# Loads without a limit in flight, and empty places that are neither gathered nor scattered, in an experts' layer

## The chip, the cores and the metric

One core of one Trainium2 chip. The time is that of the program on the device in microseconds (us). TensorE (PE in the rows; its weight loads are PEld) multiplies, VectorE (DVE), ScalarE (ACT) and GpSimd (POOL) work element by element, SyncE (SP) issues the plain DMAs, and GpSimd issues the indirect ones. Sixteen DMA engines move the bytes of all of them.

## The reference

A first block (a two-way gated delta rule beside a convolution, then a mixture of experts) and a second block (a state-space branch beside a short convolution, then a dense feed-forward), on 512 tokens of 1024 values in float32. Only the experts matter here:

```python
top_w, top_idx = ...          # 6 of 64 experts for each of 512 tokens, by the router
for e in range(64):           # for the tokens of expert e:
    y = (silu(h[tok] @ w_gate[e]) * (h[tok] @ w_up[e])) @ w_down[e]
    routed[tok] += y * weight[tok, e]
out = x + gt2 * (routed + swiglu(h, s_gate, s_up, s_down))
```

`w_gate[e]` and `w_up[e]` are 1024 x 256, `w_down[e]` is 256 x 1024, so an expert has 3 MB of weights; 512 x 6 = 3072 pairs of token and expert are computed.

## The kernel before

Normalized rows of the 512 tokens are stored in HBM (`hrow`, 640 rows), and two tables of 640 rows in HBM take the results (`yacc`: table 0 starts from x, table 1 from zeros). Rows 512 to 639 of all three stand for "no token".

The host plans 42 blocks (`plan`, L1072) of up to 128 rows. Four fixed experts (60 to 63) have a block each. The other sixty are ranked by their token count on the chip, and each rank has a capacity (`CAPS`, sum 4032): ranks 0 to 17 have blocks of their own (the first three have two each), ranks 18 to 43 share a block in pairs (64 rows each), ranks 44 to 59 in fours (32 rows each). The blocks are numbered in their order of work: 0 to 3 fixed, then fours (4, 9, 12, 14) among the largest single ones, then, from 16 to 41, a pair and a single in turn. `fixed` (L1482) and `table` (L1413) fill, for each part of a block, the list of its tokens from the front; a place that has no token gets 512 plus its row as its number and the weight 0 (L1460, L1461, L1495, L1496). Tokens over a capacity go to extra blocks in a loop with a count that is read at run time (`beyond`, L1670).

A block (`blocks`, L1641, and `ffn`, L1597): the weights of its experts are loaded in parts of 1 MB, three an expert (`load_block`, L1532; `load`, L1501; gate and up are parts 0 and 1, down is part 2). Its rows are gathered from `hrow` by one indirect DMA on GpSimd (`gather`, L1589), two blocks ahead, into one of three buffers X; these are zeroed once at the start. TensorE transposes the rows (`pt_x`), multiplies by gate and up (`gu`, 8 steps; the experts of a pair or a four run side by side on TensorE, so a block takes it as long with one expert as with four), ScalarE and VectorE make h (times the weight of the place), TensorE transposes h (`pt_h`) and multiplies by down (`py`), VectorE scales into y, and GpSimd adds y's rows to a table (`scatter`, L1633), one indirect DMA for each part, with the capacity's rows, the tables in turn. All rows of a block go through this, with or without a token. The shared expert's work is put among the blocks 10 to 16.

The weight parts go round a ring of 1 MB slots (`slot`, L1186): 10 at first, 2 more after `table`, 13 from block 17 on. SP issues the loads in program order. A load waits until its slot's last readers on TensorE are done, and also, by a dependency made by hand (L1523 to L1526, `FLIGHT = 2`), until the load before last has landed. The lines that the steps below speak of: 1522 (a weight load), 1593 (a gather), 1638 (a scatter), 139 and 142 (all matmuls and all transposes), 1217 to 1220 (zero fills), 1673 (the count of extra blocks is read), 2239 (block two reads the tables).

Of the kernel before, what the change touches and what calls it, by code (L numbers as in the profile page):

```python
# [7 lines left out]
F32 = mybir.dt.float32  # L8
# [3 lines left out]
ALU = mybir.AluOpType  # L12
# [111 lines left out]
class Tensor:  # L124


    def __init__(self, tc):
        self.tc, self.eng, self.pin, self.t = tc, tc.nc.tensor, False, 0.0
# [72 lines left out]
class ModWeights:  # L201
# [10 lines left out]
    def load(self):  # L212
        if self.todo:
            j, q = self.todo.pop(0)
            tag, bufs = self.slots[self.n % len(self.slots)]
            self.n += 1
            r = self.rows
            w = self.k.W.tile([P, r, 512], F32, tag=tag, name=f"wm{j}_{q}", bufs=bufs)
            self.k.nc.sync.dma_start(w, self.k.I["w_mod"][j, :, q * r:q * r + r, :])
            self.have.append(w)  # L220
# [24 lines left out]
def mod_vec(k, j, mw, ps, lag=2.6):  # L245
# [6 lines left out]
    t = k.W.tile([P, 4, 2], F32, tag="mt", name=f"mt{j}", bufs=2)  # L252
    nc.vector.tensor_reduce(t, pt.rearrange("p c (g s) -> p c s g", s=32)[:, :, 0:2, :], AX.X, ALU.add)
    nc.vector.tensor_tensor(k.modT[:, 4 * j:4 * j + 4, :], t,
# [803 lines left out]
        50, 49, 46, 45, 44, 44, 43, 42, 41, 41, 40, 39, 38, 37, 37, 32, 32, 32, 31, 30, 30, 28, 26, 25, 23, 22, 20, 20, 18, 17, 16]  # L1058
CAPS = [-(-c // 16) * 16 for c in CAPS]
NOV = 72  # L1060
FLIGHT = 2
LEAVE = 6
LAST = 0
AHEAD = 2
# [82 lines left out]
class Moe:  # L1147


    def __init__(self, k, es, pool):  # L1150
        self.k = k
        nc, tc = k.nc, k.tc
        self.hrow = k.dram.tile([640, 1024], F32, name="hrow")

        self.yacc = [k.dram.tile([640, 1024], F32, name=f"yacc{i}") for i in range(2)]
        self.nsc = sum(len(w) for _, _, w in BLOCKS)
        self.keep = pool(es, "moek", 1)
        self.gt2 = k.gt2 = self.keep.tile([P, 1024], F32, name="gt2")
        self.wt = {}
        self.order = []  # L1160
        self.slots = []
# [28 lines left out]
    def open_route(self, es, pool):  # L1190

        k, nc = self.k, self.k.nc
        V = nc.vector
        self.sp = pool(es, "shared", 1, side="right")
        self.er = ExitStack()
        self.rp = rp = pool(self.er, "route", 1, side="right")
        self.es = ExitStack()
        self.scp = sp = pool(self.es, "score", 1, side="right")
        keep = self.keep
        self.tok = keep.tile([P, NBT], I32, name="tok")  # L1200
        self.tw = keep.tile([P, NBT], F32, name="tw")
        self.tok2 = keep.tile([32, NB], I32, name="tok2")
        self.tok3 = keep.tile([64, NB], I32, name="tok3")
        self.tok4 = keep.tile([32, NB], I32, name="tok4")
        self.tokf = keep.tile([P, NFIX], I32, name="tokf")
        self.twf = keep.tile([P, NFIX], F32, name="twf")
        self.hs, self.Xs, self.pend = [], [], []
        self.eid = keep.tile([1, NE], I32, name="eid")
        self.eov = keep.tile([1, NOV], I32, name="eov")
        self.nov = keep.tile([1, 1], I32, name="nov")  # L1210
        self.A2 = keep.tile([P, 8], F32, name="A2")
        self.B2 = keep.tile([P, 8], F32, name="B2")
        self.rw = sp.tile([P, 8, P], F32, name="m_rw")
        nc.sync.dma_start(self.rw, k.I["router"])
        z = sp.tile([P, 1024], F32, tag="xs", name="mz", bufs=2)
        nc.gpsimd.memset(z, 0.0)
        nc.sync.dma_start(self.hrow[512:640], z)
        nc.sync.dma_start(self.yacc[0][512:640], z)
        for t in range(5):
            nc.sync.dma_start(self.yacc[1][t * P:(t + 1) * P], z)  # L1220
        c2 = rp.tile([P, 5 * P], F32, name="cst2")
        nc.sync.dma_start(c2, k.I["cst2"])
        self.iota, self.low, self.col, self.tbase, self.tcap = (c2[:, i * P:(i + 1) * P] for i in range(5))
        self.rb = sp.tile([P, NE], F32, name="rbias")
        nc.sync.dma_start(self.rb, k.I["rbias"])
        self.M = rp.tile([P, 4, NE], F32, name="M")
        self.pref = rp.tile([P, 5, NE], F32, name="pref")
        nc.gpsimd.memset(self.pref[:, 0, :], 0.0)
        self.wd = rp.tile([P, 4, NE], F32, name="wd")

        self.ohr = rp.tile([P, NE], F32, name="ohr")
        V.tensor_scalar(self.ohr, self.iota[:, 0:NE], self.col[:, 0:1], None, ALU.is_equal)
        self.iota1 = rp.tile([P, P], F32, name="iota1")
        V.tensor_scalar(self.iota1, self.iota, 1.0, None, ALU.add)

        self.tn = rp.tile([P, 4], F32, name="tn")
        for t in range(4):
            V.tensor_scalar(self.tn[:, t:t + 1], self.col[:, 0:1], float(t * P + 1), None, ALU.add)

        self.tv = rp.tile([P, 4, NFIX, 4], F32R, name="tv")  # L1240
        V.tensor_copy(self.tv, self.tn.unsqueeze(2).unsqueeze(3).to_broadcast([P, 4, NFIX, 4]))
        self.rowid = keep.tile([P, 4], I32, name="rowid")
        V.tensor_scalar(self.rowid, self.tn, -1.0, None, ALU.add)
        self.dump = keep.tile([P, 1], F32, name="dump")
        V.tensor_scalar(self.dump, self.col[:, 0:1], 513.0, None, ALU.add)
# [167 lines left out]
    def table(self, ps):  # L1413
# [57 lines left out]
        ec = rp.tile([P, 1], F32, name="tb_ec")  # L1471
        V.tensor_reduce(ec[0:NOV], le[0:NOV], AX.X, ALU.add)
        V.tensor_scalar(ec[0:NOV], ec[0:NOV], float(NE - 1), None, ALU.min)
# [27 lines left out]
    def load(self, who):  # L1501

        k, nc = self.k, self.k.nc
        if who in self.wt:
            return self.wt[who]
        kind, r = who
        if kind == "rank":
            ins, (v,) = nc.values_load_multi_w_load_instructions(self.eid[:, r:r + 1], engines=[mybir.EngineType.SP],
                                                                 min_val=0, max_val=NE - 1)
            if len(self.order) >= 8:  # L1510
                for q in ins:
                    k.tc.add_manual_dep(q.ins, self.order[-8].ins.name,
                                        mybir.DependencyInfo(mybir.DependencyClass.NoSync, mybir.DependencyReason.DATA),
                                        reason="few registers at a time")
            src = k.I["ew"][bass.ds(v, 1)].rearrange("a p f -> p (a f)")
        else:
            src = k.I["sw"] if kind == "shared" else k.I["ew"][r]
        ts = []

        def part(i):  # L1520
            t = self.slot(f"ew{kind}{r}_{i}")
            q = nc.sync.dma_start(t, src[:, 2048 * i:2048 * i + 2048])
            if len(self.order) >= FLIGHT:  # L1523
                k.tc.add_manual_dep(q.ins, self.order[-FLIGHT].ins.name,
                                    mybir.DependencyInfo(mybir.DependencyClass.Sync, mybir.DependencyReason.DATA),
                                    reason="few loads in flight, for the rows' sake")  # L1526
            self.order.append(q)
            ts.append(t)
        self.wt[who] = (ts, part)
        return self.wt[who]  # L1530
# [57 lines left out]

    def gather(self, idx):  # L1589

        X = self.Xt[0]
        self.Xt.append(self.Xt.pop(0))
        self.k.nc.gpsimd.indirect_dma_start(out=X[0:idx.shape[0]], out_offset=None, in_=self.hrow,  # L1593
                                            in_offset=bass.IndirectOffsetOnAxis(ap=idx, axis=0))
        return X

    def ffn(self, pool, ps, ws, X, wslot, n, nm):  # L1597

        k, nc = self.k, self.k.nc
        xT = pool.tile([P, 8, P], F32, tag="xT", name="xT" + nm)  # L1600
        for q in range(2):
            pt = ps.tile([P, 4, P], F32, tag="tp", name=f"pt_x{nm}{q}")
            for i in range(4):
                nc.tensor.transpose(pt[:, i, 0:n], X[0:n, (4 * q + i) * P:(4 * q + i + 1) * P], k.ident[0:n, 0:n])
            self.modulate(pt[:, :, 0:n], q, lambda c: xT[:, c, 0:n])
# [27 lines left out]
    def scatter(self, y, parts):  # L1633

        for a, idx in parts:
            n = idx.shape[0]
            self.nsc = max(self.nsc - 1, 0)
            self.k.nc.gpsimd.indirect_dma_start(out=self.yacc[self.nsc % 2], out_offset=bass.IndirectOffsetOnAxis(ap=idx, axis=0),  # L1638
                                                in_=y[a:a + n], in_offset=None, compute_op=ALU.add)

    def blocks(self, bp, ps, hooks, span):  # L1641

# [837 lines left out]
```

## Time and profile before

| | us |
|---|---|
| median of 3 runs (2093.59 to 2098.49) | 2096.74 |
| the profiled execution, its own time | 2084.69 |
| its span, first to last instruction | 2082.9 |
| TensorE busy in it | 1853.8 |
| VectorE, ScalarE, GpSimd busy | 994.3, 596.6, 501.8 |

The profile is of one execution, so sums are made in its own time and their difference is carried to the median. Busy time of an engine is an average over stages with different limits; the stage of the experts lies between about 560 and 1270 us.

### The profile page before, as it was taken

The page shows a single profiled execution, that of the slowest core. Times are in us where ns is not written, and L with a number is a line of the kernel's source. Part 1 is how long each engine was busy: PE and PEld are TensorE (multiplying, and loading weights), DVE is VectorE, ACT ScalarE, POOL GpSimd, SP SyncE. Part 2 cuts the span into 40 slices and gives each one's busy share as a digit, 9 for nine tenths or more (in the row PEclk, how much of TensorE's full clock was granted, in tenths as well). Part 3 has the DMA queues.
Part 4 walks back from the last instruction along what each step waited for, and adds up shares of the span by engine and source line. Part 5 has one row for each costly group of instructions (what it writes and reads, how often), then busy time and mean ns, then how long its engine had stood idle before and what let it go on. Part 6 is the DMA issues. An engine that isn't in the chain of part 4 may idle for free. (4 is left out here: it accounts for less than half of the span.)

```text
span 2082.9 us, 24082 instructions
## 1 busy us (share of the span) xinstructions
PE 1853.8 (89%) x8465; PEld 1244.2 (60%) x8465; DVE 994.3 (48%) x2205; ACT 596.6 (29%) x1124; POOL 501.8 (24%) x408
## 2 busy tenths in 40 slices
PE   5997698987798898988888983999999999999998
PEld 3775476875653333333322321888888878888886
DVE  4789944668764211352211215677433453323352
ACT  5443321114332111111111112533333344323341
POOL 1315334533232221212111213543100112201300
PEclk9998888999889999999999997999999999999999
DMA  7354353226589999999999996333332333233241
GB/s 301 134 184 134 95 169 90 74 86 242 188 308 339 348 357 332 338 361 369 351 339 340 367 339 206 105 95 89 101 102 86 101 117 112 89 94 101 81 142 41
DMA packets 136001, 408.53 MB, mean 196 GB/s; under 512 B 43813, under 2 KB 56229, under 8 KB 109513
## 3 DMA queue, kind: packets, MB, share of 16 engines
q1 hardware_dynamic: 110040, 365.17, 49.8%
q0 software_dynamic: 12016, 40.25, 7.7%
q10 hardware_dynamic: 13824, 1.58, 0.5%
q8 instruction: 67, 1.10, 0.2%
q14 instruction: 54, 0.43, 0.1%
HBM read 365.13 MB, written 40.63 MB: 195 GB/s over the span
## 5 line engine op out<-in xcount | busy, mean ns | idle before, releaser
L139 PE MATMUL gub<-ewrank,xTb 128*64 128x512 f32 (+5 forms) x960 | 289.4, 625 | 28.1 <-DMA ewrank<-ew 27.8
L139 PEld LDWEIGHTS gub<-ewrank,xTb 128*64 128x64 f32 (+5 forms) x960 | 94.2, 146 | 199.4 <-issue 156.1
L274 DVE TENSOR_TENSOR wlo<-wraw,whi 128x1024 fp32r<-128x1024 f32 (+1 forms) x103 | 120.8, 1173 | 139.1 <-ACT whi L273 133.7
L273 ACT CAST whi<-wraw 128x1024 fp32r<-128x1024 f32 (+1 forms) x115 | 113.9, 990 | 212.2 <-PE psi L139 50.6
L139 PE MATMUL pyb<-ewrank,hTb 128*64 128x512 f32 (+5 forms) x440 | 155.5, 602 | 5.5 <-DMA ewrank<-ew 3.4
L1616 DVE SCALAR_TENSOR_TENSOR hb<-gub,tw,sgb 128x256 f32<-128x256 f32 (+5 forms) x38 | 18.3, 482 | 274.9 <-ACT sgb L1614 274.9
L139 PE MATMUL psi<-xnh,whi 128*128 128x512 f32 (+1 forms) x368 | 141.7, 386 | 0.0
L139 PE MATMUL psi<-xnl,whi 128*128 128x512 f32 (+1 forms) x368 | 141.4, 384 | 0.0
L1638 POOL DMA_INDIRECT yacc<-yb,tok x63 | 89.0, 1413 | 179.3 <-DVE yb L1630 132.9
L1338 ACT ACTIVATE xTb<-pt_xb,B,A 128x128 f32<-128x128 f32 (+5 forms) x168 | 74.1, 445 | 174.4 <-DVE xTb L1340 173.3
L1593 POOL DMA_INDIRECT X<-hrow,tok x38 | 36.9, 972 | 338.3 <-PE pt_xb L142 332.6
L139 PE MATMUL psi<-xnh,wlo 128*128 128x512 f32 (+1 forms) x296 | 113.3, 383 | 0.0
L1340 DVE TENSOR_SCALAR xTb<-pt_xb,A,B 128x128 f32<-128x128 f32 (+5 forms) x168 | 65.5, 392 | 88.0 <-PE pt_xb L142 51.7
L1614 ACT ACTIVATE sgb<-gub 128x256 f32<-128x256 f32 (+5 forms) x42 | 16.0, 382 | 315.4 <-PE gub L139 315.4
L2403 POOL TENSOR_TENSOR fr<-fr 128x512 f32<-128x512 f32 x32 | 48.7, 1522 | 238.1 <-ACT fr L2402 238.1
L139 PE MATMUL psf<-xml,whi 128*128 128x512 f32 (+1 forms) x272 | 102.5, 377 | 0.2 <-DVE xml L274 0.2
L139 PE MATMUL psf<-xmh,whi 128*128 128x512 f32 (+1 forms) x272 | 102.4, 377 | 0.2 <-ACT xmh L273 0.2
L139 PE MATMUL psf<-xmh,wlo 128*128 128x512 f32 (+1 forms) x272 | 102.4, 377 | 0.0
L139 PEld LDWEIGHTS pyb<-ewrank,hTb 128*64 128x64 f32 (+5 forms) x440 | 46.8, 141 | 78.9 <-issue 64.1
L1630 DVE TENSOR_TENSOR yb<-pyb,gt 128x512 f32<-128x512 f32 (+5 forms) x84 | 57.9, 690 | 71.7 <-PE pyb L139 70.1
L139 PEld LDWEIGHTS psi<-xnh,whi 128*128 128x128 f32 x368 | 69.7, 190 | 14.3 <-ACT xnh L2268 0.4
L139 PEld LDWEIGHTS psi<-xnl,whi 128*128 128x128 f32 x368 | 69.9, 190 | 13.5
(752 smaller groups left out, 4032.6 us busy)
## 6 DMA issues: line engine op xcount, KB each, us to landing
ewrank<-ew SPq DMA_DIRECT2D x168, 1024.0 KB, 7.1
wraw<-w_in SPq DMA_DIRECT2D x59, 512.0 KB, 3.6
wraw<-ff SPq DMA_DIRECT2D x32, 512.0 KB, 3.5
wf<-ff SPq DMA_DIRECT2D x64, 256.0 KB, 2.7
wm<-w_mod SPq DMA_DIRECT2D x28, 512.0 KB, 7.8
ewfix<-ew SPq DMA_DIRECT2D x12, 1024.0 KB, 5.7
ewx<-ew SPq DMA_DIRECT2D x12, 1024.0 KB, 6.9
wm<-w_mod SPq DMA_DIRECT2D x10, 1024.0 KB, 5.7
```

The lines of the kernel that those rows point to most:

```text
L139: return self._done(self.eng.matmul(out, lhsT, rhs, **kw), rate, rhs)
L273: nc.scalar.copy(hi, raw)
L274: (eng or nc.vector).tensor_tensor(lo, raw, hi.bitcast(F32), ALU.subtract)
L1338: nc.scalar.activation(dst(c), pt[:, i, :], AF.Identity, scale=sa, bias=sb)
L1340: nc.vector.tensor_scalar(dst(c), pt[:, i, :], sa, sb, ALU.mult, ALU.add)
L1593: self.k.nc.gpsimd.indirect_dma_start(out=X[0:idx.shape[0]], out_offset=None, in_=self.hrow, in_offset=bass.IndirectOffsetOnAxis(ap=idx, a ...
L1614: nc.scalar.activation(sg[0:n], gu[0:n, 0:256], AF.Silu)
L1616: nc.vector.scalar_tensor_tensor(h[0:n], gu[0:n, 256:512], wslot[0:n], sg[0:n], ALU.mult, ALU.mult)
L1630: nc.vector.tensor_tensor(y[0:n, cs], py[0:n], self.gt2[0:n, cs], ALU.mult)
L1638: self.k.nc.gpsimd.indirect_dma_start(out=self.yacc[self.nsc % 2], out_offset=bass.IndirectOffsetOnAxis(ap=idx, axis=0), in_=y[a:a + n], i ...
L2403: nc.gpsimd.tensor_tensor(r, r, r, ALU.mult)
```

## The change

Three things. `FLIGHT` and the dependency made with it go, so a weight load waits for its slot alone. The gathers and scatters get a bound of 511 on their row numbers, with rows over it passed over without an error: a place without a token is neither read nor added. And `hrow` and the tables shrink to 512 rows, with which three of seven zero fills of 512 KB go.

```diff
-FLIGHT = 2
@@ __init__
-        self.hrow = k.dram.tile([640, 1024], F32, name="hrow")
-        self.yacc = [k.dram.tile([640, 1024], F32, name=f"yacc{i}") for i in range(2)]
+        self.hrow = k.dram.tile([512, 1024], F32, name="hrow")
+        self.yacc = [k.dram.tile([512, 1024], F32, name=f"yacc{i}") for i in range(2)]
@@ open_route
-        nc.sync.dma_start(self.hrow[512:640], z)
-        nc.sync.dma_start(self.yacc[0][512:640], z)
-        for t in range(5):
+        for t in range(4):
             nc.sync.dma_start(self.yacc[1][t * P:(t + 1) * P], z)
@@ load
             q = nc.sync.dma_start(t, src[:, 2048 * i:2048 * i + 2048])
-            if len(self.order) >= FLIGHT:
-                k.tc.add_manual_dep(q.ins, self.order[-FLIGHT].ins.name,
-                                    mybir.DependencyInfo(mybir.DependencyClass.Sync, mybir.DependencyReason.DATA),
-                                    reason="few loads in flight, for the rows' sake")
             self.order.append(q)
@@ gather
         self.k.nc.gpsimd.indirect_dma_start(out=X[0:idx.shape[0]], out_offset=None, in_=self.hrow,
-                                            in_offset=bass.IndirectOffsetOnAxis(ap=idx, axis=0))
+                                            in_offset=bass.IndirectOffsetOnAxis(ap=idx, axis=0),
+                                            bounds_check=511, oob_is_err=False)
@@ scatter
             self.k.nc.gpsimd.indirect_dma_start(out=self.yacc[self.nsc % 2], out_offset=bass.IndirectOffsetOnAxis(ap=idx, axis=0),
-                                                in_=y[a:a + n], in_offset=None, compute_op=ALU.add)
+                                                in_=y[a:a + n], in_offset=None, bounds_check=511, oob_is_err=False,
+                                                compute_op=ALU.add)
```

## Rows read from the trace of the kernel before

**Rows 1.** The page: slices of the span in tenths busy, and queue q0.

```profile
PE   5997698987798898988888983999999999999998
DMA  7354353226589999999999996333332333233241
...
q0 software_dynamic: 12016, 40.25, 7.7%
```

**Rows 2.** The chain that ended last: start us, us, what.

```profile
1270.09 0.11 POOLq L1673
...
1305.67 0.43 PE psi L139 x2
```

**Rows 3.** Windows: us, PE PEld DVE ACT POOL busy, PEclk, DMA share, GB/s.

```profile
809.00:1255.00 446.00, 385.47 (x1328) 139.40 (x1327) 116.75 (x314) 68.58 (x164) 82.29 (x66) 0.96 0.99 350
640.00:809.00 169.00, 152.29 (x632) 60.43 (x631) 47.60 (x162) 27.06 (x67) 38.00 (x30) 0.99 0.99 345
...
10.00:35.00 25.00, 16.07 (x104) 7.73 (x104) 12.21 (x34) 16.93 (x30) 3.70 (x11) 1.00 1.03 422
```

**Rows 4.** SP's waits from 809 to 1260 us: total us, times, longest.

```profile
SPq L1522 <- DMA ewrank<-ew: 342.4, 121, 8.7
SPq L1522 <- DMA ewx<-ew: 11.1, 4, 3.3
SPq L1522 <- PE gub L139: 3.1, 12, 0.4
```

**Rows 5.** TensorE's waits: 809 to 1260 us, then 640 to 809 us.

```profile
PE pt_hb L142 <- DVE hb L1616: 28.1, 27, 1.3
PE gub L139 <- DMA ewrank<-ew: 27.8, 17, 4.2
...
PE pyb L139 <- DMA ewrank<-ew: 1.5, 1, 1.5
```

**Rows 6.** TensorE in order of time: start, us, shape; blocks 14, 16, 36, 38, 40.

```profile
809.52 4.48 PE L139 MATMUL gub<-ewrank,xTb 128*32 128x512 f32 x34
...
828.18 1.02 PE L139 MATMUL gub<-ewx,xTb 128*32 128x512 f32 x2
...
859.29 7.09 PE L139 MATMUL gub<-ewrank,xTb 128*64 128x512 f32 x32
...
1149.37 7.09 PE L139 MATMUL gub<-ewrank,xTb 128*64 128x512 f32 x32
...
1177.13 1.08 PE L139 MATMUL gub<-ewrank,xTb 128*64 128x512 f32 x4
...
1241.83 7.09 PE L139 MATMUL gub<-ewrank,xTb 128*64 128x512 f32 x32
```

**Rows 7.** DMA queues, 587 to 595 us: packets, MB, share of 16 engines.

```profile
q1 hardware_dynamic: 315, 2.22, 66.9%
q0 software_dynamic: 304, 1.11, 34.1%
```

**Rows 8.** The same, 958 to 963 us.

```profile
q0 software_dynamic: 119, 0.46, 45.9%
```

**Rows 9.** The same, 809 to 1255 us, and its scatters' median landing.

```profile
q0 software_dynamic: 6672, 22.94, 21.0%
...
yacc<-yb,tok POOLq DMA_INDIRECT x41, 8.5
```

**Rows 10.** Page groups (busy, mean ns, idle); then GpSimd's longest wait, 809 to 1260.

```profile
L1638 POOL DMA_INDIRECT yacc<-yb,tok x63 | 89.0, 1413 | 179.3 <-DVE yb L1630 132.9
L1593 POOL DMA_INDIRECT X<-hrow,tok x38 | 36.9, 972 | 338.3 <-PE pt_xb L142 332.6
...
POOL X L1593 <- PE pt_xb L142: 257.5, 24, 24.9
```

**Rows 11.** Instructions on the zero tile: ns min/median/max, first and last start.

```profile
L1220 SPq DMA_DIRECT2D yacc<-mz x5: 319/455/524, 468.4 to 474.5; - x5
...
L1217 SPq DMA_DIRECT2D hrow<-mz x1: 383/383/383, 467.4 to 467.4; - x1
...
DMA to landing us min/median/max: 11.3/12.7/14.1
```

**Rows 12.** SP in order of time.

```profile
564.34 35.06 SPq L1522 DMA_DIRECT2D ewfix<-ew  x11
```

## The prediction

> **What bounds the kernel now.** I read the slices of the page first: for about a third of the span, from some 560 to 1260 us, the DMA engines are full while TensorE is busy too [rows 1]. That is the experts' stage, the only one that the change reaches. Then the chain of waits: it can be followed back only to 1270 us, where the count of overflow blocks is read, so what bounds the experts' stage has to be read from the stage itself; what comes behind it (scatter, reading the sums, first projections) just moves with it [rows 2]. Then busy time by stage: from 640 to 809 us TensorE is busy 152 of 169 us at nearly its full clock, and from 809 to 1255 us 385 of 446 us at a granted clock of 0.96, with the DMA share at 0.99 in both [rows 3]. In the second stretch SP waits 342 + 11 us of the 446 for an earlier load to land, in 125 waits; waits for a slot of the ring are a few us [rows 4]; that is the FLIGHT rule at work. TensorE waits for loaded weights 27.8 us in 17 waits, beside 28.1 us for VectorE's `h`, which belongs to every block [rows 5]. In 640 to 809 us there is one such wait, of 1.5 us [rows 5], so that stretch is TensorE's own and I expect nothing from it.
>
> Now the pace. After block 14, pairs of experts and single experts alternate. The pair block 16 starts its gate/up matmuls at 859.29 and the pair block 40 at 1241.83: twelve rounds of pair and single in 382.5 us, 31.9 us each. A round without a wait runs from 1149.37 to 1177.13: 27.8 us. So twelve rounds lose about 49 us to late weights, of which some 4 us are the shared expert's matmuls in the first ones: 45. The quad block 14 starts at 809.52 and has its gate/up done only near 829.2, 19.7 us instead of the 7.1 us of a block that waits for nothing: 12.6 us more [rows 6]. These sums exceed the 27.8 us of waits, since behind long ones TensorE is granted the lower of its two clocks, 1.2 instead of 2.4 GHz, for a while: that is what the 0.96 of the stretch says [rows 3]. **All that faster weights can give is 45 + 12.6 = 58 us.** The DMA side is the bound here: loads and rows together fill the engines.
>
> **Part one, FLIGHT removed.** Every load loses its wait for the load before last, SP's 354 us of waiting [rows 4] turns into waiting for ring slots (10 to 13 of 1 MB), and up to about ten loads can be queued. This adds no bytes and only pays where engines now stand idle. The share is 0.99 in the stretch; with loads alone, in 10 to 35 us, it reaches 1.03 at 422 GB/s (packets overlap a little) [rows 3]. So at most 4% of 446 us, 17 us, is idle that deeper queueing can fill; at least nothing. I take half, 9 us, because a scatter's own packets need not overlap as plain loads do. What is queued on SP behind a load that waits for a slot is more loads and then block two's first weights, which the chain needs only at 1305 us [rows 2]; nobody on the path waits for them. The fixed experts' loads, eleven of them spread over 35 us from 564 us on [rows 12], become a burst; TensorE shows no wait for them now, so their earlier landing gives nothing. The burst lies behind the last stores of hrow on SP; if it came ahead of them, eight loads at 2.5 us (1 MB at 422 GB/s, [rows 3]) would delay the first gather, and block 0, by up to 20 us. I take 0, as those stores are older in the program.
>
> **Part two, rows without a token.** Before, a block gathers all its rows: 4768 in all by the plan, and scatters 4544 (4 x 128 and the sum of CAPS, 4032). There are 512 x 6 = 3072 real ones. The reference's routing, computed for these inputs, gives the fixed experts 158 of them and the others 2914; blocks 14 to 41, those of the DMA-bound stretch, gather 3136 rows and scatter 2928, for 2132 tokens. So 1004 gathered and 796 scattered rows go there. Price of a gathered row: in 587 to 595 us queue q0 holds gathers alone: 34.1% of 16 engines for 8 us, 43.6 engine-us for 1.11 MB, which is 271 rows: 0.161 us [rows 7]. Of a scattered row, which reads and writes: in 958 to 963 us, 45.9% of 16 x 5 us for 0.46 MB, 112 rows: 0.328 us [rows 8]. Check: 3136 x 0.161 + 2928 x 0.328 is 1465 engine-us, 92 us of 16 engines; the stretch shows 21.0% of 446 us, 94 us [rows 9]. Removed: 1004 x 0.161 + 796 x 0.328 = 423 engine-us, **26 us** if it is spread over all 16 engines.
>
> Sum: 446 - 26 - 9 = 411 us for the stretch, against 446 - 58 = 388 us that TensorE needs. The DMA engines stay the later of the two (about 29.4 us a round against 27.8), so the whole 35 us counts, and what is late next is still weights, by some 2 us a round.
>
> **Small terms.** The bounds check's cost on GpSimd is in no row. Its instructions take 0.97 us (gather) and 1.41 us (scatter) [rows 10]; were each twice as long, GpSimd, busy 82 of 446 us [rows 3], would still mostly wait. Its gathers wait for a free X buffer 257 us in 24 waits [rows 10], and TensorE has no wait for X among its waits [rows 5]. Only the last scatter lies on the path: between -0.3 us (fewer descriptors to write) and +1.4 us; I take 0. The three dropped zero fills (one of hrow, one of yacc0, one of yacc1's five) are issued at 467 to 475 us in about 0.4 to 0.5 us of SP each and land in 11 to 14 us with nobody waiting [rows 11]; what covers them is the mixing stage's TensorE work, and without cover they would be worth 1.4 us of SP. I take 0. TensorE, ScalarE and VectorE still process all rows of a block, so nothing changes there; a row that isn't gathered holds older values and its weight is zero.
>
> **The number.** The profiled execution took 2084.69 us (span 2082.9), 12 us below the median of the runs shown, 2096.74. I take the 35 us off the median: **2062 us**; a profile of it should show a span near 2048. Own range: rows 26 with slack 0 to 17, and a few us for the order of work: 2050 to 2076; TensorE's limit, 58 us, is 2039.
>
> **Rival 1: front-filled parts.** `table` fills every expert's places from the front, so the empty rows are the last ones of a part. If an engine serves a run of neighbouring rows, the engines with the first runs keep every row that they have now, and only the others get lighter. A load is complete when its last engine is, and each engine carries an equal share of every load, so the pace stays that of the fullest engine: the 26 us are off the page and not off the time. What remains is the slack: 2097 - 9 = 2088 us (2080 to 2097). The trace of before can't speak for or against it: all its rows move, and a packet's engine isn't shown. The Trainium skill (DMA: Bandwidth & Descriptors, section "Why a DMA increments its semaphore by 16 and not by 1") says of some direct copies on the software path that each engine takes a run of neighbouring partitions, the first run on the lowest-numbered one; by that rule 2088 us would be the result, and no run here yet shows whether an indirect DMA does so.
>
> **Rival 2: it doesn't do what it says.** A skipped row still costs its slot (a descriptor to a dummy place), and the 0.99 share is already all that a mix of loads and scatters allows. Then neither part pays: 2097 us, give or take 4. For it: that share leaves little room. Against it: 16 engines at 0.99 still move only 350 GB/s where loads alone move 422 [rows 3].
>
> **Rival 3, slower: rows queue behind loads.** Place: the scatters, which alternate between two tables, each waiting for the one before it on its table. They land in 8.5 us now [rows 9]. If a row had to wait for all loads issued before it, seven more loads in flight at 2.5 us each would make that 26 us. Three scatters a round on two tables need 1.5 landings, 38 us against 31.9: twelve rounds lose 78 us, 2175 us. It decides from a landing of 31.9 / 1.5 = 21 us on. Against it, strongly: while both queues had work, in 587 to 595 us, q0 moved 1.11 MB in 4 KB rows and q1 2.22 MB in 8 KB rows, 271 each: one for one [rows 7]. A deeper q1 leaves a row's turn where it was.
>
> **How the numbers follow.** Forecast 0.47, rival 1 0.32, rival 2 0.13, rival 3 0.08. Under 0.2%, about 4 us, a change of this kernel can't be told from none. Faster: 0.47 and four fifths of rival 1's 0.32, together 0.72. Same: the rest of rival 1 and rival 2, 0.20. Slower: 0.08. The range takes in rival 1 and half of rival 2, and leaves out rival 3 and a little at the low end: 2046 to 2096.
>
> **What would show it.** Right: q0 of the page falls from 40.25 MB [rows 1] by 3168 rows of 4 KB, 13 MB, to about 27; SP's waits of the load line are for TensorE, no longer for DMA; the round shortens to about 29.4 us and TensorE's waits for weights to under 15 us. Rival 1: q0 falls likewise, but the DMA share drops to about 0.93 and rounds stay above 31 us with the same waits for weights. Rival 2: q0 keeps its 40 MB or its 21% of the stretch. Rival 3: scatters land later than 21 us and VectorE or GpSimd waits for them. Wrong altogether would be a shorter or longer time whose difference lies outside 640 to 1270 us, for instance through another order of work on TensorE or SP.

## The result: 2031 us, less than forecast, and the profile after

The changed kernel takes 2031.05 us, median of 4 runs (2029.70 to 2032.14), against 2096.89 us for the kernel before on the same chip: a ratio of 0.9697 (0.9669 to 0.9725), 66 us less. The sign was right; the time lies 31 us under the forecast and 15 us under the low end of the range.

The profiled execution of the changed kernel took 2032.14 us, 52.6 us less than the one before. The other 13 us of the 66 come from the execution that I had read: it was a short one of its kernel. A second profile of the kernel before, below, took 2102.56 us.

The page of the changed kernel, with queue q0, the groups that answer to [rows 10], TensorE's gate/up group, and the issues with their median us to landing:

```profile
q0 software_dynamic: 12016, 27.29, 5.5%
...
L139 PE MATMUL gub<-ewrank,xTb 128*64 128x512 f32 (+5 forms) x960 | 266.4, 595 | 0.8 <-DMA ewrank<-ew 0.2
...
L1633 POOL DMA_INDIRECT yacc<-yb,tok x63 | 89.0, 1412 | 171.3 <-DVE yb L1625 121.5
...
L1587 POOL DMA_INDIRECT X<-hrow,tok x38 | 39.5, 1041 | 292.0 <-PE pt_xb L142 286.4
...
ewrank<-ew SPq DMA_DIRECT2D x168, 1024.0 KB, 25.1
```

Queue q0 moves 27.29 MB where it moved 40.25 [rows 1], but in as many packets: in the trace the packet of a place without a token is still there, with 4 bytes (gather, 1696 more of these than before) or 8 (scatter, 1472). A load now lands 25.1 us after its issue, so about eight are in flight at 3.2 us a load.

The same stretch of both kernels, cut at 1200 us because the stage now ends earlier (columns as in [rows 3]); first before, then after:

```profile
809.00:1200.00 391.00, 338.44 (x1163) 122.80 (x1161) 104.92 (x289) 59.09 (x141) 75.65 (x61) 0.97 0.99 351
```

```profile
809.00:1200.00 391.00, 354.46 (x1266) 131.80 (x1255) 115.09 (x310) 67.09 (x161) 83.04 (x65) 0.99 1.00 370
```

TensorE gets 16 us more done in the same 391 us, at a granted clock of 0.99 instead of 0.97. The DMA share has hardly moved, 0.99 to 1.00, and yet the engines move 370 GB/s instead of 351, with fewer row bytes among them. That share is where the prediction went wrong.

Waits after, SP's from 640 to 1210 us and then TensorE's from 560 to 1260 us (total us, times, longest):

```profile
SPq L1519 <- DMA ewrank<-ew: 275.4, 117, 4.4
SPq L1519 <- PE gub L139: 81.6, 39, 16.0
SPq L1519 <- PE pyb L139: 36.2, 14, 7.6
```

```profile
PE pt_hb L142 <- DVE hb L1611: 48.4, 40, 6.5
...
PE pyb L139 <- DMA ewrank<-ew: 1.3, 3, 0.7
...
PE gub L139 <- DMA ewrank<-ew: 0.2, 1, 0.2
```

TensorE's 27.8 us of waiting for gate/up weights [rows 5] are gone. SP still waits mostly for DMA, not for TensorE: by the semaphores in the trace its DMAs use eight of them in turn, so a load waits for the DMA eight before it: from 900 to 1180 us it is issued a median of 0.12 us after that one has landed. The change lifts the limit from two to eight, not to the size of the ring.

TensorE in order of time after; the lines answer to those of [rows 6]: block 14, block 16, then three later pairs and block 40.

```profile
802.82 4.06 PE L139 MATMUL gub<-ewrank,xTb 128*32 128x512 f32 x35
...
840.09 7.09 PE L139 MATMUL gub<-ewrank,xTb 128*64 128x512 f32 x32
...
1042.81 7.09 PE L139 MATMUL gub<-ewrank,xTb 128*64 128x512 f32 x32
...
1071.30 8.29 PE L139 MATMUL gub<-ewrank,xTb 128*64 128x512 f32 x32
...
1100.71 8.29 PE L139 MATMUL gub<-ewrank,xTb 128*64 128x512 f32 x32
...
1187.98 7.09 PE L139 MATMUL gub<-ewrank,xTb 128*64 128x512 f32 x32
```

From block 16 to block 40 twelve rounds take 347.9 us, 29.0 each, where they took 382.5. Most rounds up to 1071 us take TensorE's own 27.9 (1014.95 to 1042.81); the last four take 29.2 on average, with the pair's gate/up at about 8.29 us instead of 7.09 though the granted clock there is 1.00. In the trace the fifth of the 8 steps there starts for one expert of the pair alone, and the other's follows after about 0.13 us of idle time, so that they run out of step to the end; without any rows (below) gate/up stays at 7.09. I read it as the second expert's weights coming late by a little. From block 14 to block 16 it takes 37.3 us instead of 49.8.

### The profile page after: what moved, and what is told of

Its sections match the earlier page's. It is cut to its first block, busy times and chain, and to the rows that moved or that the text cites. A ratio compares the mean times of both kernels' runs of the same rounds, so it can differ in the third digit from the quotient of the medians.

```text
span 2030.3 us, 24186 instructions
## 1 busy us (share of the span) xinstructions
PE 1827.9 (90%) x8465; PEld 1235.3 (61%) x8465; DVE 995.1 (49%) x2205; ACT 596.5 (29%) x1124; POOL 503.4 (25%) x408
## 3 DMA queue, kind: packets, MB, share of 16 engines
q0 software_dynamic: 12016, 27.29, 5.5%
## 5 line engine op out<-in xcount | busy, mean ns | idle before, releaser
L139 PE MATMUL gub<-ewrank,xTb 128*64 128x512 f32 (+5 forms) x960 | 266.4, 595 | 0.8 <-DMA ewrank<-ew 0.2
L139 PEld LDWEIGHTS gub<-ewrank,xTb 128*64 128x64 f32 (+5 forms) x960 | 89.0, 140 | 159.5 <-issue 146.7
L1633 POOL DMA_INDIRECT yacc<-yb,tok x63 | 89.0, 1412 | 171.3 <-DVE yb L1625 121.5
L1587 POOL DMA_INDIRECT X<-hrow,tok x38 | 39.5, 1041 | 292.0 <-PE pt_xb L142 286.4
## 6 DMA issues: line engine op xcount, KB each, us to landing
ewrank<-ew SPq DMA_DIRECT2D x168, 1024.0 KB, 25.1
```

The costliest lines, as they stand in the source:

```text
L139: return self._done(self.eng.matmul(out, lhsT, rhs, **kw), rate, rhs)
```

## Experiments

Where it isn't said otherwise, a kernel is the one before with one edit, times are medians, and a ratio is to the kernel before, measured beside it. Profile rows of a kernel are of 809 to 1200 us: the windows row (last three columns PEclk, DMA share, GB/s), and the queues or landings of that stretch.

**Each part alone.** Depth alone takes away only the dependency:

```diff
-            if len(self.order) >= FLIGHT:
-                k.tc.add_manual_dep(q.ins, self.order[-FLIGHT].ins.name, ...)
```

> The kernel before with FLIGHT and its dependency taken out, all rows still moved. Theory of bytes (the rows removed carry the gain, the queue was full anyway): 2080 to 2092 us, TensorE's waits for weights stay above 15 us. Theory of depth (with two loads in flight each load waits for the engine that has the most rows just then, and a deeper queue lets the engines run out of step): 2035 to 2055 us, with most waits for weights gone. If the two only work together: some 2065 to 2080 us.

Measured 2036.07 us, ratio 0.9707 (0.9670 to 0.9743).

```profile
809.00:1200.00 391.00, 353.52 (x1258) 132.05 (x1248) 113.44 (x306) 65.24 (x156) 81.50 (x65) 0.99 1.02 380
...
q1 hardware_dynamic: 17596, 126.09, 79.8%
q0 software_dynamic: 6514, 22.36, 22.2%
...
ewrank<-ew SPq DMA_DIRECT2D x117, 1024.0 KB, 25.6
...
yacc<-yb,tok POOLq DMA_INDIRECT x41, 8.7
```

With every row still moved, depth gives 59 us, where the whole change gives 66. The share rises only from 0.99 to 1.02, but the loads from 116.09 to 126.09 MB. The queues of the kernel before:

```profile
q1 hardware_dynamic: 16222, 116.09, 77.5%
q0 software_dynamic: 6097, 21.04, 21.6%
```

Rows alone is the changed kernel with the limit put back; it was measured twice.

```diff
+FLIGHT = 2
+            if len(self.order) >= FLIGHT:
+                k.tc.add_manual_dep(q.ins, self.order[-FLIGHT].ins.name, ...)
```

> The changed kernel with FLIGHT = 2 put back: places without a token are not moved, two loads in flight. Theory of bytes: 2040 to 2060 us. Theory of depth (the engines with the first rows of each part keep all they had): 2075 to 2092 us. Together only: 2065 to 2080 us.

> The rows-only kernel again, beside the last one on the same chip: 2084 us, within 6.

Measured 2084.26 us, ratio 0.9944 (0.9910 to 0.9978), and 2084.77 us, ratio 0.9935 (0.9905 to 0.9965): 11 and 13 us less than before.

```profile
809.00:1200.00 391.00, 338.32 (x1140) 122.84 (x1140) 106.43 (x291) 59.71 (x143) 77.05 (x61) 0.97 0.95 330
...
q1 hardware_dynamic: 16012, 114.48, 79.4%
q0 software_dynamic: 5969, 14.31, 15.5%
```

The rows are off the engines (15.5% of them instead of 21.6%), and the loads take nothing of what came free: 114.48 MB in the stretch where the kernel before has 116.09.

**How far executions of one kernel differ.** The kernel before, profiled again.

> The kernel before unchanged, profiled once more: its first profile took 12 us less than its median. If that profile was a lucky one, this one shows 2090 to 2098 us with more than 27.8 us of waits of TensorE for weights between 809 and 1260 us; if profiling itself shortens it, again about 2085 us.

Measured 2102.56 us in this one execution, 17.9 us longer than its first profile.

```profile
809.00:1200.00 391.00, 335.41 (x1137) 123.01 (x1137) 102.95 (x285) 57.90 (x138) 71.87 (x59) 0.96 0.98 341
```

Its rounds from block 16 to block 40 take 395.3 us instead of 382.5: 12.8 of the 17.9 us are there. With two loads in flight the pace itself varies. Each kernel with two in flight and more than 14% of rows (below) was run ten times or more and spreads over 17 us and more, and four runs with 7.9% spread over 18; the changed kernel's four spread over 2.4.

**How many loads in flight.** `FLIGHT = 1` and `FLIGHT = 3` in the kernel before, and the changed kernel with the dependency and `FLIGHT = 4`.

```diff
-FLIGHT = 2
+FLIGHT = 1
@@ the second kernel
+FLIGHT = 3
@@ the changed kernel
+FLIGHT = 4
+            if len(self.order) >= FLIGHT:
+                k.tc.add_manual_dep(q.ins, self.order[-FLIGHT].ins.name, ...)
```

> The kernel before with FLIGHT = 1: a load is issued when the last has landed. It shows the landing of a load alone: 2.45 us of transfer plus the fixed part. Theory of the gap: 4.6 to 5.2 us (with rows between), so 195 loads take 900 to 1000 us against 700 and the time is 2280 to 2400 us. Theory of the fullest engine: about 3.5 us, little above what two in flight give now, and under 2150 us.

> The kernel before with FLIGHT = 3, all rows moved. Theory of the gap: three loads in flight are 7.35 us of transfer against a fixed 2.3 us, which covers it: 2036 to 2050 us. Theory of the fullest engine: one load of lag is not enough against bursts of 8 rows an engine, 2055 to 2075 us.

> The changed kernel with FLIGHT = 4: as many loads in flight as half of what the ring lets through. Theory of bytes: the same as with FLIGHT = 2 within 5 us. Theory of depth: most of the way from that to 2031 us, since four loads already let an engine lag by two.

Measured 2432.67 us (one load, one execution), 2041.81 (three, ratio 0.9736, 0.9683 to 0.9789) and 2033.38 (four, without the empty rows, 0.9697, 0.9659 to 0.9734). One, then three in flight:

```profile
809.00:1200.00 391.00, 276.77 (x820) 93.76 (x822) 77.46 (x227) 35.57 (x85) 53.12 (x42) 0.87 0.71 231
...
ewrank<-ew SPq DMA_DIRECT2D x65, 1024.0 KB, 4.9
```

```profile
809.00:1200.00 391.00, 348.20 (x1216) 130.43 (x1209) 111.46 (x302) 64.04 (x154) 80.06 (x64) 0.99 1.02 372
...
ewrank<-ew SPq DMA_DIRECT2D x114, 1024.0 KB, 9.8
```

With all rows, one, two, three and eight in flight give 231, 351, 372 and 380 GB/s, and 2433, 2095, 2042 and 2036 us. A lone load lands in 4.9 us, of which its bytes need 2.5 (1 MB at 422 GB/s, [rows 3]). Rows are not the rest: 49 of these loads have no row's packet beside them in the trace, and they land in 4.8 us, with 1.0 us before the first packet, 3.5 us from there to the end of the last, and 0.3 us after it. That rest is what other loads must cover. The step from two to three is most of the gain; the theory that the engine with the most rows sets the pace, which allowed no such loss at one in flight, falls as the only cause. The theory of latency had 2280 to 2400 us for it, and is exceeded by 33.

**Two loads in flight without rows.** Gathers and scatters are not issued, with `FLIGHT = 2` and without the limit.

```diff
-        self.k.nc.gpsimd.indirect_dma_start(out=X[0:idx.shape[0]], ...)
-            self.k.nc.gpsimd.indirect_dma_start(out=self.yacc[self.nsc % 2], ...)
```

> The kernel before with no gather and no scatter at all (the experts' part of the output is left out), two loads in flight; TensorE does all its work on zero rows. Why do two loads in flight not fill the engines? Theory of the gap (every load has a fixed time from issue to landing beside its transfer, some 2.3 of 7.2 us, and two loads don't cover it): without rows the landing is still near 7 us and a load takes 3.3 to 3.6 us, so rounds stay near 30 us and the time 2070 to 2095 us. Theory of the fullest engine (rows lie unevenly on the engines and each load waits for the worst): without rows a load takes 2.5 us, TensorE is the bound and the time is 2025 to 2035 us.

> The same without rows and without FLIGHT. Both theories: TensorE is the bound, 2020 to 2032 us, some 5 us under the changed kernel at most, as rows no longer take the engines' time.

Measured 2017.48 us (ratio 0.9621, 0.9553 to 0.9689) and 2015.38 (0.9611, 0.9543 to 0.9680). Two in flight:

```profile
809.00:1200.00 391.00, 356.31 (x1266) 132.91 (x1264) 116.08 (x312) 67.37 (x161) 0.00 (x0) 0.99 0.84 325
...
ewrank<-ew SPq DMA_DIRECT2D x116, 1024.0 KB, 5.1
```

SP's waits without the limit, from 640 to 1210 us:

```profile
SPq L1522 <- PE gub L139: 195.5, 57, 16.7
SPq L1522 <- PE pyb L139: 149.2, 29, 9.4
SPq L1522 <- DMA ewrank<-ew: 29.4, 18, 2.8
```

Without rows depth is worth 2 us: the engines idle for a sixth of the stretch and TensorE waits for no weights. So latency alone, which I had as the theory here, isn't enough either; it takes rows beside the loads. Here SP's waits do turn to TensorE, 345 of these three rows' 374 us: with 2015 us, 16 less than the changed kernel, TensorE is the bound.

**Are the rows unevenly spread?** Capacities cut to the counts of these inputs, rounded up to 16, and gathers made for each part, so that all engines lose rows, and not only some of them if each serves a run of neighbouring rows.

```diff
-CAPS = [-(-c // 16) * 16 for c in CAPS]
+CAPS = [240, 176, 160, 96, ...]
@@ gather
+        for a, idx in self.parts(n):
+            ... out=X[a:a + idx.shape[0]] ...
```

> The kernel before with FLIGHT = 2 and no bounds check, its capacities cut to these inputs' token counts, rounded up to 16, and every part gathered by itself with its capacity's rows. Blocks 14 to 41 then move 2416 rows each way instead of 3136 and 2928, all of them real transfers that are dealt out evenly to the 16 engines: 18 us of all engines less by the rows' prices, where the bounds check took away 26 us by the same prices. If it matters which engines get lighter: this saves 18 us or more, 2076 us or less, more than the rows-only kernel's 10 us. If with two loads in flight the rows' bytes hardly matter: about as little as there, 2080 to 2092 us.

The row counts in that text are wrong: 656 gathered and 448 scattered rows fewer go in the stretch, 15.8 us by the prices of [rows 7, 8], not 18. Measured 2087.64 us, ratio 0.9952 (0.9925 to 0.9980).

```profile
809.00:1200.00 391.00, 330.08 (x1121) 114.75 (x1114) 102.61 (x285) 56.56 (x138) 80.91 (x70) 0.95 0.98 335
...
q0 software_dynamic: 5183, 16.59, 18.6%
```

As little as with rows cut at the end of a part (2084.77 us, measured beside it). How the cut lies on the engines doesn't show, but this doesn't rule out that it matters: by their intervals the even cut saves 4 to 16 us of its 15.8, the other 7 to 20 of its 26.

**Which rows.** Two in flight, scatters taken out, or gathers taken out: one of the two indirect DMAs of the diff above.

> The kernel before with its gathers and without its scatters (the experts' part of the output is left out), two loads in flight. Without any rows a load took 2.70 us where TensorE's need is 3.09, with all rows 3.57. If rows cost what their engine time is, gathers add 0.25 us a load: 2.95 us, TensorE stays the bound, 2016 to 2022 us. If every burst of rows, whatever it moves, makes the two loads miss each other, gathers bring back a good part: 2035 us or more.

> The same with the scatters and without the gathers: TensorE works on zero rows, and zeros are added to the tables. By engine time scatters add 0.48 us a load: 3.2 us, just over TensorE's need, 2020 to 2035 us. If it is the scatters that two loads in flight can't live with (each row is read and written back), nearly all of the loss returns: 2060 us or more.

Measured 2024.81 us with gathers alone (ratio 0.9677, 0.9607 to 0.9747) and 2077.61 with scatters alone (0.9928, 0.9889 to 0.9966). Gathers alone, then scatters alone:

```profile
809.00:1200.00 391.00, 356.22 (x1278) 133.14 (x1271) 116.80 (x313) 67.56 (x162) 22.34 (x24) 0.99 0.96 360
...
q0 software_dynamic: 3013, 10.77, 8.4%
```

```profile
809.00:1200.00 391.00, 335.61 (x1154) 122.47 (x1148) 105.89 (x290) 59.39 (x142) 52.15 (x37) 0.97 0.95 328
...
q1 hardware_dynamic: 16414, 117.47, 80.5%
q0 software_dynamic: 3147, 10.40, 14.4%
```

This looked as if scatters were the cause. But a row's packet holds its engine for 0.328 us when it is added and 0.159 us when it is gathered (medians of these two traces), so about the same bytes hold the engines 14.4% of the time instead of 8.4%. Kind and amount had to be told apart.

**Kind or amount.** Scatters that write in place of adding, alone and beside the gathers; then gathers issued twice without scatters; then all gathers with half of the written scatters.

```diff
-                                                in_=y[a:a + n], in_offset=None, compute_op=ALU.add)
+                                                in_=y[a:a + n], in_offset=None)
@@ gather, for the kernel with gathers twice
         self.k.nc.gpsimd.indirect_dma_start(out=X[0:idx.shape[0]], ...)
+        self.k.nc.gpsimd.indirect_dma_start(out=X[0:idx.shape[0]], ...)
@@ scatter, for half of the written scatters
+            if self.nsc % 2 == 0:
+                ... out=self.yacc[self.nsc // 2 % 2] ...
```

> The kernel before without its gathers, with two loads in flight, and with scatters that write their rows in place of adding them (so the sums are not formed). Theory A: what two loads in flight can't live with is that an added row is read and written back, 0.33 us on its engine; a written row should cost about what a gathered one does, 0.16 us, and the time should come near that of the kernel with gathers alone, 2024.81 us (2018 to 2040), with TensorE waiting for no gate/up weights. Theory B: any row written from SBUF to the tables does it, added or not; then the time stays near the kernel with scatters alone, 2077.61 us (2065 to 2090), with some 25 us of such waits.

> The kernel before, all gathers and scatters kept and two loads in flight, with scatters that write their rows in place of adding them (so the sums are not formed). Theory A (the read before the write back is what costs): 2020 to 2050 us, and TensorE's waits for gate/up weights under 10 us. Theory B (any written row costs so): 2080 to 2100 us, waits of 25 us or more as before.

> The kernel before without its scatters, two loads in flight, each gather issued twice into the same buffer (the second reads the same rows again once the first has landed). Theory A (amount): it is the engines' time for rows of any kind, and with two loads in flight the loss sets in between 8.4% of the engines' time (gathers alone, 2024.81 us) and 14.4% (added rows alone 2077.61 us, gathered and written rows 2078.35 us). Twice the gathers are some 17% of the engines: 2070 to 2090 us, and 25 us or more of TensorE's waits for gate/up weights. Theory B (kind): rows that are written to the tables are needed for it; gathers alone, however many, leave 2020 to 2040 us.

> The kernel before with all gathers and two loads in flight, with every second scatter left out and the others writing their rows in place of adding them (the sums are not formed). The rows take some 12% of the engines' time in the stretch. Theory A (amount): between the two, 2035 to 2070 us, with 5 to 20 us of TensorE's waits for gate/up weights. Theory B (kind: gathers and written rows at once): 2065 to 2080 us, as with all rows written.

Measured 2024.72 us (ratio 0.9659, 0.9587 to 0.9732), 2078.35 (0.9928, 0.9894 to 0.9961), 2074.26 (0.9925, 0.9890 to 0.9961) and 2049.29 (0.9845, 0.9784 to 0.9906). The queue rows, in this order:

```profile
q0 software_dynamic: 3536, 11.67, 7.9%
```

```profile
q1 hardware_dynamic: 16066, 114.92, 80.3%
q0 software_dynamic: 5962, 20.47, 14.4%
```

```profile
q1 hardware_dynamic: 16362, 117.05, 81.1%
q0 software_dynamic: 6114, 21.90, 16.6%
```

```profile
q1 hardware_dynamic: 16885, 120.79, 82.8%
q0 software_dynamic: 4514, 15.67, 11.7%
```

Written scatters alone cost little (2025 us against 2017 without rows), and neither "added" nor "written" explains the pair that followed: with gathers beside them the loss is back, and gathers alone do it too when there are twice as many. In order of the share of the engines that the rows take in the stretch, with two loads in flight:

| rows | share of engines | us |
|---|---|---|
| none | 0% | 2017 |
| scatters, written | 7.9% | 2025 |
| gathers | 8.4% | 2025 |
| gathers, half the scatters written | 11.7% | 2049 |
| gathers, scatters written | 14.4% | 2078 |
| scatters, added | 14.4% | 2078 |
| rows with a token only | 15.5% | 2084 |
| gathers twice | 16.6% | 2074 |
| all, capacities cut | 18.6% | 2088 |
| all, the kernel before | 21.6% | 2092 to 2098 |

The amount decides, nearly: little loss up to about 8%, 53 us from there to 14%, and some 17 us more over the next 7%, where gathers twice are 10 us out of order. The number of packets doesn't: 3147 in the stretch (added scatters) lose as much as 5962 (gathers and written scatters) at the same 14.4%. The rows that the change leaves out lie on the flat end of this.

## Why the prediction was too high, point by point

**The bound and its limit were read rightly.** The time comes out of the stretch from 809 us on, where weights were late. Between the profiles, 34.6 us are in the twelve rounds (cap 45), 12.5 from block 14 to 16 (cap 12.6), 6.7 before block 14: 2.2 up to block 0, which moves by 8 us between two profiles of the kernel before, and 4.5 between block 0 and block 14, where I had expected nothing. Behind block 40 it takes 1.2 us longer. Of the 58 us that TensorE allowed, 47 came. The median falls below "2039" because that limit was taken off the median while its 58 us were read in a short execution.

**The failed step is part one, FLIGHT.** I turned a share of 0.99 against 1.03 into "at most 17 us is idle" and took 9. Depth alone gives 59. A share of 0.99 didn't mean that the engines were doing all they could. First, packets overlap on some engines while others have none: fewer than 16 packets were in progress for 13% of the time from 809 to 1200 us before, for 0.2% with depth. Second, the median load packet takes 0.309 us in every kernel, but the mean was 0.340 in the kernel before and 0.321 with depth (packets of 8 KB from 790 to 1200 us in the trace); what holds the longer ones up isn't shown, and the mean alone doesn't set the time, for with gathers alone it is 0.341 at 2025 us. The row had the answer beside the share: 350 GB/s against 422 [rows 3]. I even wrote that down, against rival 2, and did not carry it into the sum. What I should have summed: of the 391 us to 1200, 116 MB of loads at 422 GB/s need 275 us and the rows, 21.6% of the engines, 84 us. That is 359 us, and leaves 32 us in that stretch alone where I had 17 for the longer one. With depth alone the same sum gives 386 of the 391 us, so by it the engines are nearly full there. Depth got more than these 32 us: TensorE's granted clock rose with it, from 0.97 to 0.99, and the loads ran ahead before the stretch began (below).

**Part two was mis-sized in the other direction.** 26 us were expected; rows alone give 11 to 13, and on top of depth 5 (2036.07 to 2031.05, not measured side by side; 2033.38 with four in flight, beside the 2036.07). Alone, because with two in flight the loads don't use what the rows leave; behind depth, because TensorE is the later in most rounds. What the 5 us are can be seen: rounds of the 27.9 us kind last until 1071 us with the rows cut, and in the kernel with depth alone the pairs' gate/up begins to lengthen at 960 us (TensorE in order of time):

```profile
932.99 7.09 PE L139 MATMUL gub<-ewrank,xTb 128*64 128x512 f32 x32
960.86 7.59 PE L139 MATMUL gub<-ewrank,xTb 128*64 128x512 f32 x32
```

**"The DMA engines stay the later of the two, about 29.4 us a round"** holds for the last four rounds, 29.2 us. Before them the ring, now filled ahead, lets TensorE run at its own 27.9. SP's waits from 640 to 809 us show it, the longest one before, then two after:

```profile
SPq L1522 <- DMA ewrank<-ew: 116.0, 37, 5.4
```

```profile
SPq L1519 <- PE gub L139: 71.1, 17, 16.0
SPq L1519 <- PE pyb L139: 31.9, 7, 7.6
```

After the change SP waits there for slots, because the ring is full; from 809 us on it waits for DMA. I had called that earlier stretch TensorE's own and had no term for a ring that is full at the end of it and then runs down slowly.

**Rival 1** is borne out in how rows lie on the engines, as far as one gather shows it, and is not what set the changed kernel's time. The first gather of a fixed block reads the rows of 16 tokens of 128 places:

```profile
577.95 1.13 POOL L1587 DMA_INDIRECT X<-hrow,tokf  x1 [7.33 <-issue]
```

Its 16 packets of 4 KB start in the trace in four groups of four, from 582.4, 582.9, 583.4 and 583.9 us on. The trace doesn't name engines; the step of 0.47 us is a row's 0.159 and a load packet's 0.315 us, so it reads as four engines with four rows each, in turn with loads, and the other twelve with none. The section of the Trainium skill that I cited (DMA: Bandwidth & Descriptors, section "Why a DMA increments its semaphore by 16 and not by 1") speaks of some direct copies; this indirect gather agrees with it in that few engines take the first rows. The 2088 us of rival 1 lie near the 2084 of rows alone, but its 9 us were to come from depth, which gave 59. Whether the uneven rows hold rows alone back stays open (the even cut, above).

**Rival 2** is out on both counts: skipped rows move 4 or 8 bytes, and the 0.99 could be bettered. **Rival 3** is out: scatters land in 8.5 us in 809 to 1200 us after (8.4 before), which fits rows that take turns with the loads' packets however many loads are queued.

**The signs.** q0 at 27.29 MB, waits for weights under 15 us: as told. The round of 29.4 us came out at 29.0. SP's waits turned to TensorE only up to 809 us; behind that they are for the DMA eight before. **Small terms**: a gather instruction takes 1041 ns instead of 972 and a scatter 1412 instead of 1413 [rows 10], with no wait for X on TensorE; zero was right.

What stays open is why two loads in flight lose so much between 8% and 14% of rows and so little after. One idea is that engines drift apart, so that a load waits for its last engine while others have nothing queued. It fits the lone load, whose packets take 3.5 us from first to last where its bytes need 2.5, and the times with fewer than 16 packets in progress: 29% of the stretch with rows alone, against 0.2% with depth. But no row here shows single engines, so it isn't shown.

## What to carry to other kernels

A busy share near 1 of the DMA engines is not their throughput: compare the GB/s with a stretch of loads alone (the loads' bytes at that rate, plus the engines' time for rows) before putting a ceiling on what more loads in flight can give. In this kernel three or four 1 MB loads in flight were needed where gathers and scatters took more than about a tenth of the engines; two were nearly enough beside fewer. Taking bytes out of a stretch helps only the limit that holds there, so settle first whether it is bandwidth or loads in flight.

## What was not expected of the hardware

A place that is passed over by the bound stays in the queue as a packet of 4 bytes (gather) or 8 (added row): 12016 packets before and after. A row of 4 KB held its engine for a median of 0.159 us when it was gathered or written and 0.328 us when added, so an added row costs as much as two others. The passed-over packet's median is 0.009 us. And SP's plain DMAs were limited to eight in flight by their semaphores: without any rows and without the limit by hand SP still waited 29 us for loads to land.
